# Sums of gated pairs on VectorE, an order laid out slot by slot, and four accumulators of the down product, in a hybrid decoder layer

## The chip, the core and the metric

The kernel runs on one core of one Trainium2 chip. The metric is the device time of one execution in microseconds. Three timed executions of the kernel before gave 2177.37, 2174.46 and 2172.34 us; the median is 2174.46 us.

The engines are named as in the profile: PE is TensorE (PEld its weight loads), DVE is VectorE, ACT is ScalarE, POOL is GpSimd, SP is the queue of SyncE that issues most loads. Each engine works through its own list of instructions in the order in which the program issued them; a wait on one instruction holds everything behind it on that engine.

## The reference, cut to what matters

One decoder layer on 512 positions of width 2048, in float32: an input projection, attention heads and state-space heads side by side, an output projection, and then the feed-forward part:

```python
x = x + jnp.concatenate([attn, ssm], axis=-1) @ w_out
h = rms_norm(x, norm2_w)
u = causal_dwconv(h @ w_up, ffn_conv_w, ffn_conv_b)      # w_up: 2048 x 11264
u_gate, u_val = jnp.split(u, 2, axis=-1)
return x + (jax.nn.silu(u_gate) * u_val) @ w_down        # w_down: 5632 x 2048
```

The change touches the last three lines alone: the up product with its convolution and gate, and the down product that is added to x.

## The kernel before, in words

Both products of the feed-forward part are done by a seven-product scheme for two-by-two blocks (Strassen's, in Winograd's form). A block of weights and a block of activations are cut in four, sums of the quarters are formed, and seven products P1 to P7 of the sums replace eight. Each factor is split in a high and a low part, and a product is made of three kinds of matmul: high by high (line 1265), high by low (1266) and low by high (1268).

**Groups, items, slots.** The up product has 44 groups (one of 128 gate columns with the 128 value columns that belong to them), the down product 24: three passes (over 8, 7 and 7 pairs of hidden blocks) of eight groups. A group has seven items, P1 to P7, and all items stand in one list, in which two groups are interleaved: P5 of group g, P3 of g-1, P1 of g, P4 of g-1, P6 of g, P2 of g, P7 of g. The place in that list is the slot. An item has 24 matmuls of 128x256 where the group works over 8 blocks (the up product and the first pass of the down product), and 21 where it works over 7.

**What a slot does.** The main loop issues an item's matmuls, then what reads its product out of PSUM (`up_after` or `down_after`), and then what the table `events` holds for that slot (`run`), the high part of the item three slots on (`split`, ScalarE, line 1038), the low part of the item two slots on (`split_lo`, VectorE, line 1047), and one step of the gate's work (`side`). So the order on each engine is set by the slot numbers given to `at`, and within a slot by the order of these calls.

**Sums of weights.** Per group the four quarters "11", "12", "21" and "22" of the weights are loaded (SP's queue, line 1007; quarter 22 a second time as "22b"), into two buffers `rawb` (for 21) and four buffers `rawa`. VectorE makes s1 = 21 + 22 (line 1021), s2 = s1 - 11 (1025) and s4 = 12 - s2 (1027) in the PSUM tile `s`; GpSimd makes s3 = 11 - 21 in place in `rawb` (line 1014). P5 is made from s1, P6 from s2, P3 from s4, P7 from s3; P1, P2 and P4 from 11, 12 and 22b. With p5 the slot of the group's P5, s1 is issued in slot p5-5, s3 in p5-2, s2 in p5 and s4 in p5+4.

**Gate's work.** Per up group VectorE scales the product rows (`ug`, `uv`, lines 1192 and 1193), runs the convolution (line 1174, with a first step on ScalarE, 1173) and multiplies gate and value into half of the tile `gt` (line 1185). After every second group, when `gt` holds a pair of hidden blocks, GpSimd makes the pair's four sums in three instructions (`sums`, lines 879 to 881) and stores the tile in `gd` in DRAM (line 1190).

**Down product.** Each pass first loads the pair sums back from `gd` (`b_load`, GpSimd's queue, line 1077, into the tiles `ld`; three buffers in the first pass, six later) and splits them in high and low parts `cmb` (`b_split`: ScalarE 1088, VectorE 1089), fourteen times per pass in the first sixteen slots counted from `base`, the P5 of the group ahead of the pass. `down_after` adds each product into the accumulator `acc_s` of the group (line 1144). The accumulator is loaded by GpSimd's queue (`down_acc`) from x (`x2d`, line 1206) or from what the pass before stored (`pd`, line 1208), one slot ahead of the group's P5, into one of two buffers, and stored (line 1053) one slot after the group's P4.

## Time and profile before

| | |
|---|---|
| median of the three times | 2174.46 us (2172.34 to 2177.37) |
| profiled execution, own time | 2176.35 us |
| its span, first to last instruction | 2174.7 us |
| PE, PEld busy | 2096.7 us (96%), 1966.4 us (90%) |
| DVE busy | 1645.8 us (76%) |
| ACT busy | 985.7 us (45%) |
| POOL busy | 363.0 us (17%) |
| mean granted TensorE clock | 0.989 of full speed |

The profiled execution is 1.65 us longer than its span, and 1.9 us above the median. The shares are averages over stages with different limits: the first 820 us are the mixer, the next 840 us the up product, the last 500 us the down product. Rows of a timeline give the start, the duration, the engine, line and operation, out<-in with the shape, and, in brackets, how long the engine had been idle before it and what released it. An instruction's recorded duration overlaps the next one's by some 0.08 us on VectorE; what it takes of the engine's time is read from start to start. Some matmul records are missing, so counts of them serve as shares, not as exact numbers.

### The profile page before, as it was taken

Reading aid. Unit: us, or ns where it says so; the run is one execution under the profiler, and the core shown is the slowest. Engines: PE = TensorE matmul, PEld = TensorE weight load, DVE = VectorE, ACT = ScalarE, POOL = GpSimd, SP = SyncE. Lnnn points to the kernel's source line nnn. Section 1 sums busy time; section 2 is a strip of 40 time slices with the busy share of each in tenths; the row PEclk is TensorE's granted clock in tenths of the full one; section 3 lists DMA queues with packets and bytes.
Section 4 is the critical chain, followed back from the end, with each engine's and each line's share of the span. In section 5 each row is a group of like instructions: output and inputs, shape, how many; then the busy total and the mean of one; then the engine's idle time right before and its main releaser. Section 6 shows DMA issues by size and latency. Waiting matters only on the chain.

```text
span 2174.7 us, 37764 instructions
## 1 busy us (share of the span) xinstructions
PE 2096.7 (96%) x15366; PEld 1966.4 (90%) x15366; DVE 1645.8 (76%) x2185; ACT 985.7 (45%) x1433; POOL 363.0 (17%) x293
## 2 busy tenths in 40 slices
PE   9999999999999989999999999999999899899798
PEld 7988888888888879999999999999999799899798
DVE  6545555345655559999999999999999867877776
ACT  5433445334444445544454554544455433434432
POOL 0010000000000011222212212222232322213111
PEclk9999999999999999999999999999999999999999
DMA  5232222232225444444444444444445556657553
GB/s 195 75 106 86 77 79 78 88 107 88 68 97 180 160 168 146 167 154 165 165 146 167 154 162 159 158 153 165 155 163 206 209 186 224 220 207 238 194 195 125
DMA packets 97406, 328.20 MB, mean 151 GB/s; under 512 B 10704, under 2 KB 15120, under 8 KB 94416
## 3 DMA queue, kind: packets, MB, share of 16 engines
q1 hardware_dynamic: 81424, 257.36, 34.9%
q0 software_dynamic: 15808, 68.43, 8.5%
q8 instruction: 121, 1.98, 0.4%
q14 instruction: 53, 0.43, 0.1%
HBM read 283.77 MB, written 41.98 MB: 150 GB/s over the span
## 4 chain that ended last, share of the span: by engine, by line
PE 72%; issue 12%; DVE 9%; DMA 3%; POOL 3%; ACT 1%; POOLq 0%; SPq 0%; DVEq 0%; ACTq 0%
PE acc L184 29%; PE x L1268 12%; PE x L1265 12%; PE x L1266 11%; PE sm L184 4%; DVE lo L1047 4%; POOL rawb L1014 1%; PE y L1266 1%; PE y L1265 1%; PE y L1268 1%; DVE s L1027 1%; DVE ug L1192 1%; DVE cmb L1089 1%; DMA acc_s<-pd 1%; DMA pd<-acc_s 1%
## 5 line engine op out<-in xcount | busy, mean ns | idle before, releaser
L1265 PE MATMUL x<-cmb,hi 128*128 128x256 f32 x3168 | 764.1, 281 | 26.0 <-DVE acc_s L1144 20.8
L1266 PE MATMUL x<-cmb,hi 128*128 128x256 f32 x3168 | 761.9, 281 | 8.7 <-DVE cmb L1089 8.3
L1265 PEld LDWEIGHTS x<-cmb,hi 128*128 128x128 f32 x3168 | 604.8, 191 | 29.2 <-issue 17.7
L1266 PEld LDWEIGHTS x<-cmb,hi 128*128 128x128 f32 x3168 | 605.4, 191 | 10.1 <-DVE cmb L1089 9.3
L1268 PE MATMUL x<-cmb,lo 128*128 128x256 f32 x3168 | 442.6, 282 | 30.6 <-DVE lo L1047 30.1
L1268 PEld LDWEIGHTS x<-cmb,lo 128*128 128x128 f32 x3168 | 401.9, 191 | 38.7 <-DVE lo L1047 38.5
L184 DVE TENSOR_TENSOR lo<-raw,hi 128x512 fp32r<-128x512 f32 (+1 forms) x240 | 164.4, 691 | 246.7 <-ACT hi L184 232.1
L184 PE MATMUL acc<-A,hi 128*128 128x512 f32 x704 | 281.1, 399 | 0.9 <-ACT hi L184 0.9
L1038 ACT ACTIVATE hi<-s 128x1024 fp32r<-128x1024 f32 (+1 forms) x201 | 200.8, 999 | 171.0 <-DVE s L1025 60.7
L184 PE MATMUL acc<-A,lo 128*128 128x512 f32 x704 | 277.7, 395 | 0.1
L1038 ACT ACTIVATE hi<-rawa 128x1024 fp32r<-128x1024 f32 (+1 forms) x204 | 210.5, 1032 | 146.6 <-PE x L1266 133.7
L184 PE MATMUL acc<-B,hi 128*128 128x512 f32 x704 | 276.9, 393 | 0.0
L184 ACT ACTIVATE hi<-raw 128x512 fp32r<-128x512 f32 (+1 forms) x240 | 150.3, 629 | 261.5 <-PE acc L184 228.5
L1047 DVE TENSOR_TENSOR lo<-rawa,hi 128x1024 fp32r<-128x1024 f32 (+1 forms) x204 | 251.1, 1231 | 0.0
L1014 POOL TENSOR_TENSOR rawb<-rawa,rawb 128x1024 f32<-128x1024 f32 (+1 forms) x68 | 160.9, 2367 | 465.8 <-DMA rawa<-wu 216.3
L1047 DVE TENSOR_TENSOR lo<-s,hi 128x1024 fp32r<-128x1024 f32 (+1 forms) x201 | 237.2, 1180 | 0.0
L1155 ACT ACTIVATE cP<-x 128x256 f32<-128x256 f32 x132 | 50.9, 385 | 318.4 <-PE x L1268 318.4
L184 PEld LDWEIGHTS acc<-A,lo 128*128 128x128 f32 x704 | 132.1, 188 | 32.4 <-DVE lo L184 1.5
L184 PEld LDWEIGHTS acc<-A,hi 128*128 128x128 f32 x704 | 132.7, 188 | 29.1 <-ACT hi L184 1.3
L184 PEld LDWEIGHTS acc<-B,hi 128*128 128x128 f32 x704 | 132.5, 188 | 28.7 <-DVE B L184 0.4
L1144 DVE TENSOR_TENSOR acc_s<-x,acc_s 128x256 f32<-128x256 f32 x144 | 60.8, 422 | 117.7 <-PE x L1268 56.1
L1047 DVE TENSOR_TENSOR lo<-rawb,hi 128x1024 fp32r<-128x1024 f32 (+1 forms) x68 | 137.3, 2019 | 0.0
(209 smaller groups left out, 3071.4 us busy)
## 6 DMA issues: line engine op xcount, KB each, us to landing
rawa<-wu SPq DMA_DIRECT2D x176, 512.0 KB, 4.1
raw<-wi SPq DMA_DIRECT2D x79, 512.0 KB, 3.5
rawa<-wdb SPq DMA_DIRECT2D x64, 448.0 KB, 4.2
rawb<-wu SPq DMA_DIRECT2D x44, 512.0 KB, 3.3
gd<-gt POOLq DMA_DIRECT2D x22, 1024.0 KB, 4.2
raw<-wo SPq DMA_DIRECT2D x32, 512.0 KB, 3.3
rawa<-wda SPq DMA_DIRECT2D x32, 512.0 KB, 4.2
ld<-gd POOLq DMA_DIRECT2D x26, 512.0 KB, 6.2
```

The costliest lines, as they stand in the source:

```text
L184: return fn(out, *args, **kw)
L1014: po.tensor_tensor(r, raw[gi, "11"][:, :n], r, op=OP.subtract)
L1027: ve.tensor_tensor(s_, raw[gi, "12"][:, :n], s_, op=OP.subtract)
L1038: se.activation(h[:, :n], src[:, :n], AF.Copy)
L1047: ve.tensor_tensor(l[:, :n], src[:, :n], h[:, :n].bitcast(F32), op=OP.subtract)
L1089: ve.tensor_tensor(lo, ld[:, :m, :], hi.bitcast(F32), op=OP.subtract)
L1144: ve.tensor_tensor(a[:, row, half], src, a[:, row, half], op=op)
L1155: se.activation(g[x], X[:, 256:] if x == "P5" else X[:, :256], AF.Copy)
L1192: yield lambda: ve.tensor_tensor(ug[:, 2:514], ug[:, 2:514], rbc, op=OP.mult)
L1265: pe.matmul(out, w, bk[:, 0, q, :], start=fresh and q == 0, stop=False, skip_group_check=True)
L1266: pe.matmul(out, w, bk[:, 1, q, :], start=False, stop=False, skip_group_check=True)
L1268: pe.matmul(out, l[:, q * 128:(q + 1) * 128], bk[:, 0, q, :], start=False, stop=q == n - 1, skip_group_check=True)
```

## The change

It moves the three instructions of the pair sums from GpSimd to VectorE, in two parts in different slots. Gate steps no longer come from a list of which one is taken per slot; each has a slot of its own. A second table `after` is run later in the slot: a slot now runs `events`, then the low part (`split_lo`), then `after` (s1, s3, `b_split`, the gate's steps, the pair sums), then the high part (`split`). s1 and s3 of a group stand together in slot p5-3, s4 in p5+5. In the down product all groups from the third on take their accumulator from four buffers `acc` in another pool, loaded in slot p5-6 (p5-2 for the third); the first and second keep `acc_s`, loaded in p5-2 and p5-5. The `ld` tiles of the second and third pass are five instead of six.

```diff
-    def sums(E, g):
-        E.tensor_tensor(g[:, 4:6, :], g[:, 1:4:2, :], g[:, 0:2, :], op=OP.subtract)
-        E.tensor_tensor(g[:, 6, :], g[:, 3, :], g[:, 4, :], op=OP.subtract)
-        E.tensor_tensor(g[:, 7, :], g[:, 2, :], g[:, 6, :], op=OP.subtract)
+    def sums(E, g, part=None):
+        if part != 1:
+            E.tensor_tensor(g[:, 4:6, :], g[:, 1:4:2, :], g[:, 0:2, :], op=OP.subtract)
+        if part != 0:
+            E.tensor_tensor(g[:, 6, :], g[:, 3, :], g[:, 4, :], op=OP.subtract)
+            E.tensor_tensor(g[:, 7, :], g[:, 2, :], g[:, 6, :], op=OP.subtract)
...
-        at(p5 - 5 if gi != 1 else 0, add, gi, "s1"), at(pos[gi, "P7"] - 8 if gi else -3, add, gi, "s3")
-        at(max(p5 - 1, p6 - 4), add, gi, "s2"), at(p6, add, gi, "s4")
+        if gi:
+            at(p5 - 3 if gi > 1 else 1, add, gi, "s1", where=after)
+            at(p5 - 3 if gi > 1 else 1, add, gi, "s3", where=after)
+        else:
+            at(-5, add, gi, "s1"), at(-3, add, gi, "s3")
+        at(max(p5 - 1, p6 - 4), add, gi, "s2"), at(pos[gi, "P3"] - 3, add, gi, "s4")
...
-        box["depth"] = 6
+        box["depth"] = 5
...
-        early = 5 if p == 0 else 6
+        early = 5
         for q in range(14):
-            at(base + slots[q], b_split, k0 + q)
+            at(base + slots[q], b_split, k0 + q, where=after)
         for q in range(14):
-            at(base - 6 + q // 2 if q < early else base + slots[q - early if p else q - 3] + 1, b_load, k0 + q)
+            at(base - 6 + q // 2 if q < early else base + slots[q - (5 if p else 3)] + 1, b_load, k0 + q)
         if p == 0:
-            at(base + 21, down_pool)
+            at(base + 19, down_pool)
...
-                sums(po, box["gt"])
+        def t_sums(n):
+            sums(ve, box["gt"], n)
+            if n:
...
                 po.dma_start(gd[p][:, pr - PASSES[p][0]], box["gt"])
...
+        t0 = pos[i, "P4"]
+        for d, fn in ((0, lambda: ve.tensor_tensor(ug[:, 2:514], ug[:, 2:514], rbc, op=OP.mult)),
+                      (1, lambda: ve.tensor_tensor(uv[:, 258:514], uv[:, 258:514], rbc[:, 256:], op=OP.mult)),
+                      (3, lambda: conv(ug, i, "tg", 0)), (4, lambda: conv(ug, i, "tg", 1)), (5, val0),
+                      (6, lambda: conv(uv, NF + i, "tv", 1)), (6, last)):
+            at(t0 + d, fn, where=after)
+        if i % 2:
+            at(t0 + 7, t_sums, 0, where=after), at(t0 + (10 if i < NF - 1 else 8), t_sums, 1, where=after)
...
-        a = g["acc"] = side_tile(lp, [2, S], "acc_s", 2)
+        if gi < NF + 2:
+            a = g["acc"] = side_tile(lp, [2, S], "acc_s", 2)
+        else:
+            a = g["acc"] = side_tile(box["pool"], [2, S], "acc", 4)
...
-            at(pos[gi, "P5"] - 1, down_acc, gi)
+            p5 = pos[gi, "P5"]
+            at(p5 - 2 if gi == NF else p5 - 5 if gi == NF + 1 else p5 - 2 if gi == NF + 2 else p5 - 6, down_acc, gi)
...
+    def step_slot(slot):
+        run(slot)
+        if slot > -3:
+            split_lo(slot + 2)
+        run(slot, after)
+        split(slot + 3)
```

The first place is VectorE's list in the up product, after a pair of groups is complete. Before, from the product that fills `gt` (the tiles `lo`, `hi`, `rawa`, `rawb` and `s` are those of the weights, `ug`, `uv`, `tg`, `tv` those of the gate, `x` and `y` the PSUM products):

```order
L1185 TENSOR_TENSOR gt<-tg,tv 128x512
L1163 TENSOR_TENSOR uv_7164<-x,rbc 128x256
L1047 TENSOR_TENSOR lo_11013<-rawa,hi_10980 128x1024
L1192 TENSOR_TENSOR ug_7162<-ug_7162,rbc 128x512
L1027 TENSOR_TENSOR s<-rawa,s 128x1024
L1047 TENSOR_TENSOR lo_11047<-rawb,hi_11011 128x1024
L1193 TENSOR_TENSOR uv_7164<-uv_7164,rbc 128x256
L1157 TENSOR_TENSOR ug_7158<-y,cP_10974 128x256
L1047 TENSOR_TENSOR lo_11081<-s,hi_11045 128x1024
```

And in the changed kernel, from the first of the pair's sums on (line 880; 882 and 883 are the other two, 1023 is s1, 1029 is s4, 1049 the low part):

```order
L880 TENSOR_TENSOR gt<-gt 128x512
L1201 TENSOR_TENSOR ug_7158<-ug_7158,rbc 128x512
L1049 TENSOR_TENSOR lo_11278<-rawb,hi_11248 128x1024
L1023 TENSOR_TENSOR s<-rawb,rawa 128x1024
L1202 TENSOR_TENSOR uv_7160<-uv_7160,rbc 128x256
L1163 TENSOR_TENSOR ug_7162<-y,cP_11209 128x256
L1029 TENSOR_TENSOR s<-rawa,s 128x1024
L1049 TENSOR_TENSOR lo_11315<-s,hi_11284 128x1024
L1165 TENSOR_TENSOR uv_7164<-x,cP_11144 128x256
L1049 TENSOR_TENSOR lo_11348<-s,hi_11317 128x1024
L882 TENSOR_TENSOR gt<-gt 128x256
L883 TENSOR_TENSOR gt<-gt 128x256
```

The sums are new in this list. s1 (1023) now stands right ahead of the short product of `uv` and of a run of instructions that read `y`, `x` or `s`, which are PSUM tiles; s3, which GpSimd can start once s1 has read `rawb`, falls beside that run.

The second place is VectorE's list where the up product ends and the first pass of the down product begins, in the slot of the first down group's P6. Before and, in the second fence, in the changed kernel (`cmb<-ld` is `b_split`, 1089 and now 1096; the accumulator's lines are 1144 and now 1150):

```order
L1144 TENSOR_TENSOR acc_s<-x,acc_s 128x256
L1027 TENSOR_TENSOR s<-rawa,s 128x1024
L1089 TENSOR_TENSOR cmb_17735<-ld,cmb_17735 128x1024 x2
L1047 TENSOR_TENSOR lo_17744<-rawb,hi_17702 128x1024
L1193 TENSOR_TENSOR uv_7164<-uv_7164,rbc 128x256
```

```order
L1150 TENSOR_TENSOR acc_s<-x,acc_s 128x256
L1049 TENSOR_TENSOR lo_17737<-rawb,hi_17706 128x1024
L1023 TENSOR_TENSOR s<-rawb,rawa 128x1024
L1096 TENSOR_TENSOR cmb_17742<-ld,cmb_17742 128x1024 x2
L1202 TENSOR_TENSOR uv_7164<-uv_7164,rbc 128x256
```

The low part of a later item now comes ahead of the two splits of loaded sums, not behind them, and s1 stands between.

The third place is GpSimd's list in the first pass of the down product (`x2d_148` and `x2d_149` are loaded into the accumulator of the fifth group; `pd_2` is the store of the third). Before:

```order
L1053 DMA pd_1_7059<-acc_s 128x1024
L1014 TENSOR_TENSOR rawb<-rawa,rawb 128x1024
L1206 DMA acc_s<-x2d_146 128x512
L1206 DMA acc_s<-x2d_147 128x512
L1053 DMA pd_2_7060<-acc_s 128x1024
L1014 TENSOR_TENSOR rawb<-rawa,rawb 128x1024
L1206 DMA acc_s<-x2d_148 128x512
L1206 DMA acc_s<-x2d_149 128x512
```

In the changed kernel:

```order
L1218 DMA acc<-x2d_146 128x512
L1218 DMA acc<-x2d_147 128x512
L1056 DMA pd_1_7059<-acc_s 128x1024
L1016 TENSOR_TENSOR rawb<-rawa,rawb 128x1024
L1218 DMA acc<-x2d_148 128x512
L1218 DMA acc<-x2d_149 128x512
L1056 DMA pd_2_7060<-acc 128x1024
L1016 TENSOR_TENSOR rawb<-rawa,rawb 128x1024
```

An accumulator's load now stands ahead of the store and of the sum that were issued before it, and goes into a buffer of its own rather than into the one that the store has just been issued from.

More of the change, by code (lines that the diff above doesn't have):

```diff
@@ L1048, in split_lo, with at @@
         parts[k] = (h, l)
-    events = {}
-    def at(slot, fn, *args):
-        events.setdefault(slot, []).append(lambda: fn(*args))
+    events, after = {}, {}
+    def at(slot, fn, *args, where=events):
+        where.setdefault(slot, []).append(lambda: fn(*args))
     for gi in range(len(groups)):
@@ L1128, in body @@
         at(slot, x_split, n)
-    side = []
     box = {}
@@ L1163, in up_after @@
             ve.tensor_tensor(uv[:, 2:258], X[:, :256], rbc[:, :256], op=OP.mult)
-            side.extend(up_side(i, ug, uv))
+            up_side(i, ug, uv)
     def up_side(i, ug, uv):
@@ L1230, in body, with run @@
     at(1, lambda: stat_bc(box["ps"].tile([128, 512], F32, name="y")))
-    def run(slot):
-        for fn in events.pop(slot, ()):
-            fn()
-    def before(lo, hi):
-        for slot in range(lo, hi):
-            run(slot)
-            split(slot + 3)
-            if slot > -3:
-                split_lo(slot + 2)
+    def run(slot, where=events):
+        for fn in where.pop(slot, ()):
+            fn()
+    def step_slot(slot):
[4 more added lines that the diff above has]
+        split(slot + 3)
     for slot in range(min(events), -3):
         run(slot)
-    before(-3, -2)
+    step_slot(-3)
     while gens:
@@ L1250, in body @@
                                                reuse_waits="tile"))
-    before(-2, 0)
+    step_slot(-2), step_slot(-1)
     for k, (gi, x) in enumerate(items):
@@ L1272, in body @@
         (up_after if g["ph"] == "up" else down_after)(g, x)
-        run(k)
-        split(k + 3)
-        split_lo(k + 2)
-        if side:
-            side.pop(0)()
+        step_slot(k)
     for slot in sorted(events):
```

8 lines of the change are left out of this document (removed).

## The prediction

> **What bounds the kernel now.** I first read the stages: the busy times of the engines in stretches of the span. The columns are PE, PEld, DVE, ACT and POOL busy time with their instructions, the granted TensorE clock, and DMA.
>
> ```profile
> core 0: us, PE busy (x) PEld busy (x) DVE busy (x) ACT busy (x) POOL busy (x), PEclk, DMA share, GB/s
> 905.00:1623.00 718.00, 701.66 (x6047) 698.12 (x6046) 702.67 (x757) 358.00 (x468) 168.39 (x108) 1.00 0.44 159
> 1660.00:1760.00 100.00, 81.47 (x605) 78.31 (x604) 80.34 (x89) 44.05 (x48) 31.23 (x31) 0.90 0.54 191
> 1760.00:1840.00 80.00, 80.00 (x697) 80.00 (x696) 59.10 (x70) 30.24 (x30) 21.16 (x22) 1.00 0.63 225
> 1840.00:1900.00 60.00, 52.98 (x421) 51.91 (x421) 50.03 (x60) 29.95 (x33) 14.67 (x16) 0.94 0.59 207
> 1960.00:2080.00 120.00, 107.06 (x874) 104.66 (x873) 92.41 (x113) 50.27 (x56) 30.42 (x32) 0.97 0.65 222
> ```
>
> The stretch 1760 to 1840, inside the first pass of the down product, is TensorE's own pace: never idle, full clock, 697 recorded matmuls in 80 us, 0.1148 us each. At that pace 1660 to 1760 would hold 871 matmuls and held 605, so 30.5 us are lost; 1840 to 1900 holds 421, worth 48.3 us, so 11.7 are lost; 1960 to 2080 holds 874, worth 100.3, so 19.7 are lost. These are the starts of the three passes. In the up product (first row) DVE is busier than PE: 702.67 of 718 us.
>
> The pace of a group is seen in the accumulator's additions, which follow the products. Each row stands for the same product one group later (first pair: groups over 8 blocks; second: over 7).
>
> ```profile
> 1763.36 0.42 DVE L1144 TENSOR_TENSOR acc_s<-x,acc_s 128x256 f32<-128x256 f32 x1 [1.16 <-PE x L1268]
> 1782.72 0.43 DVE L1144 TENSOR_TENSOR acc_s<-x,acc_s 128x256 f32<-128x256 f32 x1 [1.16 <-PE x L1268]
> ...
> 2135.85 0.42 DVE L1144 TENSOR_TENSOR acc_s<-x,acc_s 128x256 f32<-128x256 f32 x1 [0.42 <-PE x L1268]
> 2152.79 0.43 DVE L1144 TENSOR_TENSOR acc_s<-x,acc_s 128x256 f32<-128x256 f32 x1 [0.97 <-PE x L1268]
> ```
>
> So TensorE needs 19.36 us for a group over 8 blocks (2.77 per slot) and 16.94 over 7 (2.42 per slot). VectorE waits for PE here, so nothing else sets this pace. In the up product a pair of groups could take 38.72 us. GpSimd's timeline shows what it takes, and the operations that VectorE meets:
>
> ```profile
> 905.18 1.29 POOL L879 TENSOR_TENSOR gt<-gt 128x512 f32<-128x512 f32 x1 [17.48 <-DVE gt L1185]
> ...
> 1243.83 2.41 POOL L1014 TENSOR_TENSOR rawb<-rawa,rawb 128x1024 f32<-128x1024 f32 x1 [12.01 <-ACT hi L1038]
> 1268.72 0.57 POOL L1190 DMA_DIRECT2D gd<-gt  x1 [0.30 <-POOL gt L881]
> 1269.31 2.41 POOL L1014 TENSOR_TENSOR rawb<-rawa,rawb 128x1024 f32<-128x1024 f32 x1
> ...
> 1623.40 1.29 POOL L879 TENSOR_TENSOR gt<-gt 128x512 f32<-128x512 f32 x1 [18.06 <-DVE gt L1185]
> ```
>
> From 905.18 to 1623.40 lie 18 pairs: 39.90 us each, 1.18 over TensorE's pace. VectorE's timeline of one such pair says why:
>
> ```profile
> 1243.62 1.21 DVE L1047 TENSOR_TENSOR lo<-s,hi 128x1024 fp32r<-128x1024 f32 x1
> 1244.75 2.04 DVE L1185 TENSOR_TENSOR gt<-tg,tv 128x512 f32<-128x512 f32 x1
> ...
> 1263.54 0.69 DVE L1185 TENSOR_TENSOR gt<-tg,tv 128x512 f32<-128x512 f32 x1
> 1265.08 1.60 DVE L1047 TENSOR_TENSOR lo<-rawa,hi 128x1024 fp32r<-128x1024 f32 x1
> 1266.60 1.22 DVE L1192 TENSOR_TENSOR ug<-ug,rbc 128x512 f32<-128x512 f32 x1
> 1268.88 3.93 DVE L1047 TENSOR_TENSOR lo<-rawb,hi 128x1024 fp32r<-128x1024 f32 x1
> ```
>
> The same `gt` product takes 0.69 us alone and 2.04 where GpSimd's s3 (1243.83 to 1246.24) runs; the low part of `rawb` takes 3.93 us beside the s3 at 1269.31. But the low part at 1243.62, which reads the PSUM tile `s`, keeps its 1.21 under the same s3. So GpSimd's sums stop a VectorE instruction that reads two SBUF tiles, and not one that reads PSUM.
>
> In the down product the waits say what is late; the second and third entries are VectorE's:
>
> ```profile
> PE x L1265 <- DVE acc_s L1144: 20.8, 9, 5.0
> DVE acc_s L1144 <- DMA acc_s<-pd: 33.9, 12, 4.9
> DVE acc_s L1144 <- DMA acc_s<-x2d: 18.7, 4, 8.1
> ```
>
> **The change, part by part.** *Up product.* VectorE's 702.67 us are 39.04 per pair. GpSimd's stops in the pair above are 2.04-0.69, 1.60-1.21, 1.22-0.68 and 3.93-1.21, together 5.00 us (the 0.68 is the row at 1698.56 below). Without them VectorE has 34.04 us of work. The pair sums come onto it: one 128x512, two 128x256. The nearest rows are `gt` alone (0.69) and the accumulator's 0.42, so 1.53 us; the same sums of the mixer's `gx` tiles on VectorE bound it above:
>
> ```profile
> L184 DVE TENSOR_TENSOR gx<-gx 128x512 f32<-128x512 f32 x8 | 7.6, 950 | 1.8 <-ACT gx L184 1.8
> ```
>
> That is 0.95+0.84, 1.79 us; from start to start (0.08 less each) 1.3 is the lower end. I take 1.53, since 950 ns is a mean over a place where other work interferes: 35.6 us per pair against TensorE's 38.72. VectorE no longer bounds the pair, if s3 stops nothing. In the new order s3 can start only when s1 is done; what then stands on VectorE is one product of two SBUF tiles (`uv`, L1202), then s4, two low parts and two sums that all read PSUM: about 4 us, longer than s3's 2.41. Nothing of the five microseconds is left but the `uv` product's case. When both start together, VectorE has won:
>
> ```profile
> 1698.56 0.68 DVE L1192 TENSOR_TENSOR ug<-ug,rbc 128x512 f32<-128x512 f32 x1
> 1698.57 2.92 POOL L1014 TENSOR_TENSOR rawb<-rawa,rawb 128x1024 f32<-128x1024 f32 x1
> ```
>
> It is VectorE that keeps its 0.68 and GpSimd that takes 0.5 longer. The `uv` product starts right behind s1, and GpSimd's s3 needs the message that s1 is done, so I take no stop; the ends are 0 and 2.72 us per group. Within a slot the most VectorE work is s2, a low part and a convolution step, 1.13+1.13+0.66 from start to start, 2.9 us beside a slot of 2.77, and the next slots are shorter; TensorE reads a low part only two slots on. s1 itself, two slots later than before, is ready 2.3 us after the end of P6 on TensorE, its high part 1.05 later, and TensorE wants it after two more items, 5.5 us: 2.1 us are left. So the up product should run at TensorE's pace: 18 x 1.18 = 21.2 us gained. The pair before 905 and the transition are not in this.
>
> The Trainium skill, SBUF — State Buffer, "Who interferes with whom", says that VectorE and GpSimd share a port pair by an exclusive lock and that whoever issues first has it for the whole instruction. The row at 1698.57 agrees, the row at 1268.88 does not: that low part started 0.43 us ahead of the s3 at 1269.31 and still ended after it (it had started behind the descriptor work of 1268.72, which by the page should not hold it). By the rule the `uv` product wins and the sum is as above; by that row it loses 2.72 us in every group, which is the second rival below.
>
> *Down product, accumulators.* Before, an accumulator's load waits on GpSimd's queue until the store from the same buffer has landed. In the first transition:
>
> ```profile
> 1707.67 1.09 POOL L1206 DMA_DIRECT2D acc_s<-x2d  x2
> 1716.73 0.42 DVE L1144 TENSOR_TENSOR acc_s<-x,acc_s 128x256 f32<-128x256 f32 x1 [5.04 <-DMA acc_s<-x2d]
> 1739.79 0.58 POOL L1206 DMA_DIRECT2D acc_s<-x2d  x1 [4.42 <-DMA pd<-acc_s]
> 1743.77 0.42 DVE L1144 TENSOR_TENSOR acc_s<-x,acc_s 128x256 f32<-128x256 f32 x1 [8.07 <-DMA acc_s<-x2d]
> acc_s<-x2d POOLq DMA_DIRECT2D x16, 256.0 KB, 4.2
> ```
>
> Four buffers and six slots of lead (16.6 us, or 14.5 over 7 blocks) cover even the 9.1 us from 1707.67 to 1716.73. The third group has two slots and its own item, 8.3 us, against a landing of 4.2: covered, if GpSimd comes to it in time. What queues behind the early load on GpSimd, a store and s3, does not wait longer, since the buffer is free four groups ahead. So I drop these waits. What is left of each transition is VectorE's work, which the early load doesn't touch.
>
> *First transition.* In the 17 slots from the first `b_split` to the last pair sum, the new order gives VectorE 38 instructions of 128x1024 (1.13 us from start to start), 21 of 128x256 (0.34), 9 convolution steps (0.66) and 7 others of 128x512 (0.60): 60.1 us. TensorE needs 17 x 2.77 = 47.0. VectorE falls 13.1 us behind; it may lag 2.4 (one slot less an addition) before TensorE waits; and s3 may fall between two `b_split` in a row, which read two SBUF tiles, 2.4 more. So 13.1 of the 30.5 us stay and 17.4 are gained.
>
> *The other two.* Over 7 blocks the rows are
>
> ```profile
> L1047 DVE TENSOR_TENSOR lo<-rawa,hi 128x896 fp32r<-128x896 f32 x48 | 51.9, 1082 | 0.0
> L1089 DVE TENSOR_TENSOR cmb<-ld,cmb 128x768 fp32r<-128x768 f32 x14 | 13.9, 994 | 0.0
> ```
>
> A group has ten of the first size (1.00 from start to start) and seven additions: 12.4 us. The fourteen `b_split` are 7 x 1.13 + 7 x 0.87 = 14.0, spread over two groups: 38.8 us beside TensorE's 33.9, so 4.9 behind, less 2.4 of lag, plus 2.4 for the same s3: 4.9. At the start of the second pass one of the groups still has TensorE's longer items, which I put at 1.4 us more cover: 3.5. Gained: 11.7-3.5 and 19.7-4.9, together 23.0.
>
> Everything else (five `ld` tiles for six, steps of ScalarE placed ahead of the high part, s4 a slot later) I cost at nothing: ScalarE is busy 358 of 718 us in the up product, and s4's low part is still read two slots after it. Without that cover each would be a share of an item per group, as in the last rival.
>
> The sum: 21.2+17.4+23.0 = 61.6 us off. The profiled span becomes 2113.1, its execution 2114.8; against the median of 2174.46 it is 2112.9. I say 2112.
>
> **The rivals.** *The transitions keep more* (0.15). The waits show 20.8 us of TensorE directly behind the late accumulators; the rest of the 61.9 us lost (30.5+11.7+19.7) may come from the chain of `b_load`, where a buffer freed by VectorE is loaded one or two slots ahead of use:
>
> ```profile
> POOL ld L1077 <- DVE cmb L1089: 83.1, 25, 11.5
> ```
>
> The change leaves that chain as it is in the first pass and with a buffer less in the others. Then 21.2+20.8 = 42.0 are gained: 2132. Against it, VectorE, not a load, was at work in 80.34 of the 100 us.
>
> *s3 stops the `uv` product* (0.10). With 2.72 us per group VectorE has 35.6+5.4 = 41.0 per pair, 1.1 more than today: the up product loses 20 instead of gaining 21, and the down product still gains 40.4: 2154. It decides once the stop passes 1.6 us.
>
> *The loads are early in the order and not in time* (0.05). GpSimd takes its queue in order and stands behind `b_load`s in the first transition; then 5.04 and 8.07 stay: 2125.
>
> *Slower* (0.04). s1 now stands 2.1 us ahead of need with ScalarE's high part behind it, in order. If it were late by more in each group, through its two loads or through VectorE's lag, each microsecond beyond would cost TensorE one in each of the 43 up groups that have this slot; from 3.6 us late on (1.5 x 43 = 64.5) the gain is gone: 2177. Against it, the two loads are asked for six slots ahead.
>
> **How the numbers follow.** The forecast has 0.66; its own range is 2099 (the transitions lose half of what I count) to 2124. With the first and third rival 2098 to 2142 holds a little over eight in ten; 2154 and the slower case are left out. A difference of 0.2%, 4.3 us, is about what a measurement of this kernel can tell from none. Only the last rival is slower: faster 0.94, within 0.2% 0.02, slower 0.04.
>
> **What would show it.** The stops are gone: the `gt`, `ug` and `rawb` rows at 0.69, 0.68 and 1.21, pairs 38.7 us apart, s3 about 2.6 us long and the `uv` product 0.41. A `uv` product near 3 us, or pairs at 39.9 or more, would be the second rival. In the down product the accumulator's waits for DMA vanish; the starts of the passes lose about 13, 4 and 5 us, with VectorE busy in them; ScalarE or VectorE waiting for `ld` there would be the first rival. An idle TensorE behind the high part of P5 in every up group would make the prediction wrong altogether.

## The result and the profile after

The changed kernel takes 2127.01 us (median; 2125.47 to 2128.22), the kernel before 2174.34 (2171.68 to 2177.37) beside it. The ratio is 0.9783, with a 95% interval of 0.9770 to 0.9795. The direction and the range hold, but 47 us are gained where 62 were counted.

The page of the changed kernel gives its span and busy times:

```profile
span 2125.4 us, 37670 instructions
PE 2081.9 (98%) x15366; PEld 1958.4 (92%) x15366; DVE 1584.6 (75%) x2251; ACT 987.9 (46%) x1433; POOL 283.4 (13%) x227
```

The stages of the changed kernel, with the columns of the prediction's first fence (us of the span; PE, PEld, DVE, ACT and POOL busy with instructions; granted clock; DMA share; GB/s): the up product, then the starts of the three passes.

```profile
908.00:1605.00 697.00, 697.00 (x6051) 697.00 (x6050) 650.55 (x811) 362.54 (x469) 98.40 (x54) 1.00 0.46 164
1640.00:1740.00 100.00, 86.12 (x684) 83.48 (x684) 86.52 (x104) 47.01 (x51) 27.46 (x27) 0.95 0.61 211
1820.00:1880.00 60.00, 57.07 (x485) 56.08 (x484) 53.20 (x67) 31.15 (x35) 19.37 (x19) 1.00 0.70 240
1960.00:2060.00 100.00, 95.86 (x799) 94.80 (x798) 84.43 (x106) 44.10 (x50) 25.55 (x25) 0.97 0.65 219
```

In the up product TensorE is never idle now, and VectorE is busy 650.55 of 697 us where it had been busy 702.67 of 718. The starts of the passes are still thin: at 0.1148 us a matmul the 684, 485 and 799 leave 21.5, 4.3 and 8.3 us lost.

To see where each microsecond went, I compare the start of the same VectorE instruction in two traces: the `gt` product of the second and of the twentieth pair, and the addition of P1 in the 3rd, 14th and 21st down group. VectorE's timeline of the kernel before, and then of the changed kernel:

```profile
904.43 0.67 DVE L1185 TENSOR_TENSOR gt<-tg,tv 128x512 f32<-128x512 f32 x1
1622.64 0.68 DVE L1185 TENSOR_TENSOR gt<-tg,tv 128x512 f32<-128x512 f32 x1
1749.61 0.42 DVE L1144 TENSOR_TENSOR acc_s<-x,acc_s 128x256 f32<-128x256 f32 x1 [1.68 <-PE x L1268]
1962.46 0.43 DVE L1144 TENSOR_TENSOR acc_s<-x,acc_s 128x256 f32<-128x256 f32 x1 [0.97 <-PE x L1268]
2102.05 0.42 DVE L1144 TENSOR_TENSOR acc_s<-x,acc_s 128x256 f32<-128x256 f32 x1
```

```profile
907.78 0.69 DVE L1191 TENSOR_TENSOR gt<-tg,tv 128x512 f32<-128x512 f32 x1
1604.74 0.69 DVE L1191 TENSOR_TENSOR gt<-tg,tv 128x512 f32<-128x512 f32 x1
1721.14 0.42 DVE L1150 TENSOR_TENSOR acc<-x,acc 128x256 f32<-128x256 f32 x1
1925.98 0.42 DVE L1150 TENSOR_TENSOR acc<-x,acc 128x256 f32<-128x256 f32 x1 [0.98 <-PE x L1281]
2052.76 0.42 DVE L1150 TENSOR_TENSOR acc<-x,acc 128x256 f32<-128x256 f32 x1 [0.98 <-PE x L1281]
```

Row by row the changed kernel is 3.4 us later, then 17.9, 28.5, 36.5 and 49.3 earlier. The differences of these numbers are the gains of the stages. The table has them for every kernel of this document, against the same trace of before. (Each comes from one profiled execution. At the start, traces whose order is the same there differ by up to 1.8 us, so a microsecond in that column means little; in the up product they agree within 0.1, in the first transition within 0.7. The medians were taken in five batches, with the kernel before at 2173.8 to 2176.9 us; between batches they compare to within some 3 us.)

| Gain in us | start, to 2nd pair | up, 18 pairs | first transition | second | third | median us |
|---|---|---|---|---|---|---|
| forecast | 0 | 21.2 | 17.4 | 8.2 | 14.8 | 2112 |
| the changed kernel | -3.4 | 21.3 | 10.6 | 8.0 | 12.8 | 2127.0 |
| without s3 | 0.5 | 21.3 | 13.2 | 7.9 | 15.5 | 2119.1 |
| sums on GpSimd | -2.9 | 21.3 | 5.5 | 7.9 | 13.8 | 2130.7 |
| s1, s3, s4 in old slots | -2.5 | 20.8 | 13.5 | 3.1 | 12.2 | 2130.6 |
| s1, s3 ahead of the low part | -5.2 | 0.0 | 5.9 | 4.9 | 12.6 | 2158.7 |
| second group's s1, s3 at old place | -1.1 | 21.3 | 9.9 | 6.1 | 15.7 | 2124.1 |
| three s3 behind the loads | -2.5 | 21.3 | 12.1 | 7.9 | 15.7 | 2122.7 |
| third accumulator a slot earlier | -2.3 | 21.3 | 14.4 | 4.7 | 15.7 | 2123.3 |
| these last three together | -2.0 | 21.3 | 17.6 | 7.9 | 15.7 | 2115.4 |
| sums and s1, s3, s4 as before | -2.7 | -0.8 | 8.7 | 2.8 | 12.3 | 2157.3 |
| accumulators as before | -4.0 | 21.3 | 5.2 | -19.7 | -7.7 | 2185.3 |
| only the accumulators changed | -1.8 | 0.1 | 8.0 | 7.2 | 14.7 | 2148.7 |
| three together, 4 splits doubled | -1.9 | 21.3 | 11.5 | 7.9 | 15.5 | 2121.4 |

The second line against the first: the up product and the second transition are as forecast; the first transition lacks 6.8 us, the third 2.0, and the start loses 3.4 that were not in the sum.

**The up product.** The two `gt` products of the changed kernel above, at 907.78 and 1604.74, stand 18 pairs apart: 38.72 us each. VectorE's groups by line (busy us, mean ns of one) show that the `gt` product and the `uv` product are not stopped, on the mean of all 44; one pair's timeline shows the place of s3.

```profile
L1191 DVE TENSOR_TENSOR gt<-tg,tv 128x512 f32<-128x512 f32 x44 | 30.4, 692 | 1.5
L1202 DVE TENSOR_TENSOR uv<-uv,rbc 128x256 f32<-128x256 f32 x44 | 18.4, 418 | 0.0
```

```profile
1242.88 0.42 DVE L1202 TENSOR_TENSOR uv<-uv,rbc 128x256 f32<-128x256 f32 x1
1243.12 2.45 POOL L1016 TENSOR_TENSOR rawb<-rawa,rawb 128x1024 f32<-128x1024 f32 x1 [13.29 <-DVE s L1023]
1243.59 1.22 DVE L1029 TENSOR_TENSOR s<-rawa,s 128x1024 f32<-128x1024 f32 x1
```

s3 comes 0.24 us behind the `uv` product, which keeps its 0.42; what follows on VectorE reads PSUM and keeps its 1.22.

**The start.** Here s1 and s3 of the second group stand in slot 1, and there VectorE's next but one instruction reads two SBUF tiles (timelines of VectorE and GpSimd in the changed kernel):

```profile
813.31 3.33 POOL L1016 TENSOR_TENSOR rawb<-rawa,rawb 128x1024 f32<-128x1024 f32 x1 [7.88 <-DVE s L1023]
814.30 3.42 DVE L1049 TENSOR_TENSOR lo<-rawb,hi 128x1024 fp32r<-128x1024 f32 x1
```

A low part that takes 1.22 alone takes 3.42.

**The first transition.** From the timelines of VectorE, GpSimd, ScalarE and TensorE in the changed kernel:

```profile
1677.74 2.35 DVE L1096 TENSOR_TENSOR cmb<-ld,cmb 128x1024 fp32r<-128x1024 f32 x2
1677.97 4.73 POOL L1016 TENSOR_TENSOR rawb<-rawa,rawb 128x1024 f32<-128x1024 f32 x1 [2.31 <-DVE s L1023]
1682.64 1.52 POOL L1084 DMA_DIRECT2D ld<-gd  x2
1687.80 1.06 ACT L1095 ACTIVATE cmb<-ld 128x1024 fp32r<-128x1024 f32 x1 [4.76 <-DMA ld<-gd]
1688.91 0.58 PE L1278 MATMUL x<-cmb,hi 128*128 128x256 f32 x1 [3.08 <-ACT cmb L1095]
...
1706.10 2.44 POOL L1016 TENSOR_TENSOR rawb<-rawa,rawb 128x1024 f32<-128x1024 f32 x1 [3.63 <-DVE s L1023]
1706.32 2.50 DVE L883 TENSOR_TENSOR gt<-gt 128x256 f32<-128x256 f32 x1
1709.12 0.58 POOL L1198 DMA_DIRECT2D gd<-gt  x1 [0.58 <-DVE gt L883]
1709.70 2.14 POOL L1218 DMA_DIRECT2D acc<-x2d  x4
1717.07 0.42 DVE L1150 TENSOR_TENSOR acc<-x,acc 128x256 f32<-128x256 f32 x1 [4.19 <-DMA acc<-x2d]
```

Two things are late. First, two `b_split` in a row hold s3 off: it ends at 1682.70 instead of about 1680.4, and only then come the two loads queued behind it; ScalarE waits 4.76 us for the data and TensorE 3.08 for ScalarE. Second, GpSimd comes to the third group's accumulator at 1709.70, and VectorE waits 4.19 for it. Ahead of that load stands the last store of the pair sums, and it was held up by an s3 as well: the s3 at 1706.10 stops the last pair sum, which takes 2.50 us instead of 0.42. The loads issued there then land 5.5 to 7.0 us after their issue (the view of tile `acc`, 1695 to 1730 us).

### The profile page after: what moved, and what is told of

The parts are those of the page before. It is cut to its first block, busy times and chain, and to the rows that moved or that the text cites. A ratio compares the mean times of both kernels' runs of the same rounds, so it can differ in the third digit from the quotient of the medians.

```text
span 2125.4 us, 37670 instructions
## 1 busy us (share of the span) xinstructions
PE 2081.9 (98%) x15366; PEld 1958.4 (92%) x15366; DVE 1584.6 (75%) x2251; ACT 987.9 (46%) x1433; POOL 283.4 (13%) x227
## 4 chain that ended last, share of the span: by engine, by line
PE 88%; DVE 5%; issue 3%; DMA 2%; ACT 1%; POOL 1%; POOLq 0%; SPq 0%; DVEq 0%; ACTq 0%
PE acc L184 30%; PE x L1281 16%; PE x L1279 15%; PE x L1278 15%; PE sm L184 4%; PE y L1281 2%; PE y L1278 2%; PE y L1279 2%; DVE lo L1049 1%; DMA ld<-gd 1%; DVE cmb L1096 1%; POOL rawb L1016 0%; DVE lo L184 0%; DVE s L1023 0%; DMA acc<-x2d 0%
## 5 line engine op out<-in xcount | busy, mean ns | idle before, releaser
L1281 PE MATMUL x<-cmb,lo 128*128 128x256 f32 x3168 | 436.2, 280 | 6.3 <-DVE lo L1049 6.3
L1016 POOL TENSOR_TENSOR rawb<-rawa,rawb 128x1024 f32<-128x1024 f32 (+1 forms) x68 | 169.3, 2490 | 927.1 <-DVE s L1023 723.8
L1049 DVE TENSOR_TENSOR lo<-rawa,hi 128x1024 fp32r<-128x1024 f32 (+1 forms) x204 | 241.3, 1183 | 0.0
L1040 ACT ACTIVATE hi<-rawa 128x1024 fp32r<-128x1024 f32 (+1 forms) x204 | 209.5, 1027 | 39.1 <-PE x L1279 38.9
L184 PE MATMUL acc<-hi,A 128*128 128x256 f32 (+2 forms) x448 | 135.4, 302 | 0.7 <-DVE u L184 0.7
L184 PE MATMUL acc<-lo,A 128*128 128x256 f32 (+2 forms) x448 | 133.5, 298 | 0.0
```

The source lines that it names most:

```text
L184: return fn(out, *args, **kw)
L1016: po.tensor_tensor(r, raw[gi, "11"][:, :n], r, op=OP.subtract)
L1040: se.activation(h[:, :n], src[:, :n], AF.Copy)
L1049: ve.tensor_tensor(l[:, :n], src[:, :n], h[:, :n].bitcast(F32), op=OP.subtract)
L1281: pe.matmul(out, l[:, q * 128:(q + 1) * 128], bk[:, 0, q, :], start=False, stop=q == n - 1, skip_group_check=True)
```

## The experiments

My theory of what is missing (14 us by the medians, 12 in the table): it is three collisions of the new order (s3 at the start, s3 with the loads behind it in the transitions, the third accumulator), not the terms of the sum. The rival: VectorE's own work in the transitions is more than I counted. A first group of runs takes the up product's two edits apart, a second the three collisions, a third the accumulators.

**Without s3.** It leaves out the sum s3 for all groups (P7 then multiplies another operand), so part of the computation is missing.

```diff
-            po.tensor_tensor(r, raw[gi, "11"][:, :n], r, op=OP.subtract)
```

> The changed kernel without GpSimd's s3 at all (P7 multiplies quarter 21 itself, so the output is not the reference's). Theory: in the up product's steady pairs s3 is hidden already, so pairs stay at 38.72 us; what the prediction missed (3.4 us at the start of the up product, about 6.8 us in the first transition, 2.1 in the third) is s3 meeting VectorE instructions with two SBUF inputs there, and delaying the loads queued behind it. Without s3 that comes back: 2113 to 2120 us. Rival: the transitions are longer because VectorE's own work there was counted too low; then only the directly blocked instructions come back (2.2 + 2.1 + 1.9 us) and the time is 2121 to 2125.

2119.06 us (ratio 0.9745, 0.9730 to 0.9760). The up product gains nothing by it: s3 is hidden there. The start gets 3.9 us back, the first transition 2.6 and the third 2.7, together 9.2 of the 12.2 us missing in the table. The first transition still lacks 4.2; VectorE waits 6.18 us there for the third group's accumulator.

**Sums back on GpSimd, the new order kept.**

```diff
-            sums(ve, box["gt"], n)
+            sums(po, box["gt"], n)
```

> The changed kernel with the pair sums back on GpSimd, in their new slots. Theory A (the order round s3 is what frees the pair; VectorE has 3 us to spare): the sums stop VectorE by 2.5 to 3.5 us per pair instead of costing it 1.5, 36.5 to 37.5 us of 38.72, pairs stay at 38.7 to 38.8 and the time at 2125 to 2131. Theory B (the move of the sums is what pays): pairs go back to 39.3 or more, 2138 to 2150.

2130.68 us (0.9798, 0.9784 to 0.9813). The pairs stay at 38.72, and the up product keeps its 21.3 us; the time that is lost against the changed kernel is lost in the first transition (5.5 instead of 10.6).

**The sums on VectorE, s1, s3 and s4 in their old slots.**

```diff
-            at(p5 - 3 if gi > 1 else 1, add, gi, "s1", where=after)
-            at(p5 - 3 if gi > 1 else 1, add, gi, "s3", where=after)
...
-        at(max(p5 - 1, p6 - 4), add, gi, "s2"), at(pos[gi, "P3"] - 3, add, gi, "s4")
+        at(p5 - 5 if gi != 1 else 0, add, gi, "s1"), at(pos[gi, "P7"] - 8 if gi else -3, add, gi, "s3")
+        at(max(p5 - 1, p6 - 4), add, gi, "s2"), at(p6, add, gi, "s4")
```

> The changed kernel with s1, s3 and s4 in the slots and at the place within the slot that they had before; the sums stay on VectorE. Theory A: s3 falls beside a convolution step and the gate's product again and stops VectorE 1.3 to 2.7 us per group; at 1.3 the pair needs 38.2 us of VectorE (time 2122 to 2131, since the collision at the start of the up product also goes), at 2.7 it needs 41.0 (2165). Theory B (moving the sums alone pays): 2122 to 2128, pairs at 38.72.

2130.56 us (0.9801, 0.9785 to 0.9818). Again the pairs stay at 38.7. The stage 1000 to 1600 us, first of the kernel with the sums on GpSimd, then of this one:

```profile
1000.00:1600.00 600.00, 600.00 (x5209) 600.00 (x5208) 549.99 (x652) 311.95 (x404) 125.53 (x91) 1.00 0.46 163
```

```profile
1000.00:1600.00 600.00, 600.00 (x5205) 599.88 (x5204) 590.58 (x697) 311.90 (x403) 83.39 (x46) 1.00 0.47 163
```

600 us are 15.5 pairs: VectorE needs 35.5 us per pair in the one, less than the 36.5 to 37.5 that I had expected, and 38.1 in the other. Both are under TensorE's 38.72, so both give the whole 21 us. Either edit is enough in the up product; with the new order kept, the sums on VectorE even cost it a little (36.1 in the changed kernel).

**Both undone.** The last two edits at once.

> The changed kernel with the pair sums on GpSimd and s1, s3 and s4 in their earlier slots, both undone at once; the gate's fixed slots, the low part ahead of the gate's steps and the early accumulators stay. Theory: the pair has a threshold, VectorE's need with its stops against TensorE's 38.72 us; either edit alone brings it under (the two runs with one undone have pairs of 38.7), neither leaves it above: pairs at 39.5 to 40 us again, 14 to 23 us lost against the changed kernel, 2143 to 2151. Rival: the gate's fixed slots alone are enough: pairs at 38.7, 2130 to 2134.

2157.29 us (0.9920, 0.9905 to 0.9935), the pairs at 39.94: neither edit, no gain. So the pair has a threshold, and the effects of the two edits don't add. (VectorE is busy 584.37 of the 600 us from 1000 to 1600, 38.9 us per pair, which is only 0.2 over 38.72; it also waits for TensorE's products, 12.1 us in that stretch or 0.8 per pair, and together they come near the 39.94.) I expected at most 2151; the other 6 us are lost in the transitions, 1.9 in the first and 5.2 in the second, as with s1 and s3 in their old slots alone (4.9 in the second).

**s1 and s3 one step earlier within their slot**, ahead of the low part:

```diff
-            at(p5 - 3 if gi > 1 else 1, add, gi, "s1", where=after)
-            at(p5 - 3 if gi > 1 else 1, add, gi, "s3", where=after)
+            at(p5 - 3 if gi > 1 else 1, add, gi, "s1", where=events)
+            at(p5 - 3 if gi > 1 else 1, add, gi, "s3", where=events)
```

> The changed kernel with s1 and s3 one step earlier within the same slot, ahead of the low part of rawb, so that two instructions with two SBUF inputs (the low part, 1.13 us, and the uv product, 0.34) stand behind s1 instead of one. Theory A (whoever waits gets the pair when the first instruction ends): s3 starts after the low part and the uv product is stopped for about 2.4 us per group: VectorE 40.4 us per pair, 2155 to 2170. Theory B (VectorE keeps the pair through back-to-back instructions, as it did with two splits in a row in two of three transitions): s3 takes 3.8 us instead of 2.4, nothing stops, pairs at 38.72, 2123 to 2131.

2158.71 us (0.9926, 0.9911 to 0.9941). The timelines of VectorE and GpSimd in one of its groups:

```profile
1233.40 1.22 DVE L1049 TENSOR_TENSOR lo<-rawb,hi 128x1024 fp32r<-128x1024 f32 x1
1233.63 3.25 POOL L1016 TENSOR_TENSOR rawb<-rawa,rawb 128x1024 f32<-128x1024 f32 x1 [16.67 <-DVE s L1023]
1234.54 2.62 DVE L1202 TENSOR_TENSOR uv<-uv,rbc 128x256 f32<-128x256 f32 x1
```

Now s3 meets the low part, gets its turn when that ends, and the `uv` product takes 2.62 us. (41 of the 44 take 2.62 or 2.63.) This is what the prediction's second rival describes: pairs at 39.9, the up gain gone, even with the sums on VectorE. One place within a slot is worth 21 us.

**The start.** s1 and s3 of the second group back in their earlier slots:

```diff
-            at(p5 - 3 if gi > 1 else 1, add, gi, "s1", where=after)
-            at(p5 - 3 if gi > 1 else 1, add, gi, "s3", where=after)
+            if gi > 1:
+                at(p5 - 3, add, gi, "s1", where=after)
+                at(p5 - 3, add, gi, "s3", where=after)
+            else:
+                at(0, add, gi, "s1"), at(pos[gi, "P7"] - 8, add, gi, "s3")
```

> The changed kernel with s1 and s3 of the second group back in their earlier slots (0 and eight slots ahead of P7); nothing else is changed. Theory: the 3.4 us that the changed kernel loses ahead of the first pair come from this one s3, now beside a low part of two SBUF tiles: the first pair's gt product comes about 3.4 us earlier than in the changed kernel, and the whole is about 3.4 us shorter, 2123.6. Rival: the start is lost to the order of the gate's steps there, which this edit leaves as it is: 2127, the first pair unchanged.

2124.09 us (0.9768, 0.9754 to 0.9783). The stretches 800 to 840 us of the kernel before, of the changed kernel and of this one:

```profile
800.00:820.00 20.00, 19.96 (x146) 19.72 (x146) 15.06 (x20) 11.51 (x16) 4.34 (x2) 0.82 0.68 236
820.00:840.00 20.00, 20.00 (x175) 20.00 (x175) 17.21 (x21) 9.49 (x12) 2.41 (x1) 1.00 0.38 132
```

```profile
800.00:820.00 20.00, 18.48 (x127) 18.04 (x127) 13.62 (x16) 9.05 (x12) 5.28 (x2) 0.80 0.61 201
820.00:840.00 20.00, 19.27 (x166) 19.07 (x166) 17.11 (x21) 10.07 (x14) 2.47 (x1) 1.00 0.38 129
```

```profile
800.00:820.00 20.00, 19.66 (x138) 19.22 (x138) 13.69 (x19) 11.16 (x14) 4.33 (x2) 0.81 0.69 229
820.00:840.00 20.00, 20.00 (x176) 20.00 (x175) 17.14 (x20) 9.01 (x13) 2.47 (x1) 1.00 0.40 138
```

Of 28 matmuls missing (321 before, 293 after, 3.2 us) 21 are back, 2.4 us; the `gt` product of the second pair is 2.3 us earlier, where 3.4 were expected. But this is one trace against one. The same stretch holds 304 in the two later kernels with this edit (three together, splits doubled), and 288 to 299 in the four with the changed start. By the table's first column the edit is worth 1.3 us on the mean (1.7 late against 3.0). So the theory holds for a part, and the rest of the loss stays open: the kernel with only the accumulators changed, whose order at the start is that of before, is 1.8 late as well.

**s3 behind the loads.** In the second, tenth and eighteenth down group s3 stands one slot later:

```diff
-            at(p5 - 3 if gi > 1 else 1, add, gi, "s3", where=after)
+            at(p5 - 2 if gi in (NF + 1, NF + 9, NF + 17) else p5 - 3 if gi > 1 else 1, add, gi, "s3", where=after)
```

> s3 of the second, tenth and eighteenth group of the down product one slot later, behind the loads that stood behind it on GpSimd and out of the slot with two b_split in a row; nothing else is changed. Theory: what the transitions keep beyond VectorE's work is s3 held up by the splits (4.73 us in the first) and the loads of the next sums that queue behind it; TensorE's stretch from 1680 to 1700 us of the first transition fills, 4 to 6 us in all are gained, 2121 to 2123. Rival 1: VectorE's own work sets the transition, and s3's place changes only which of its instructions is stopped: 2126 to 2128. Rival 2: s3 one slot later makes P7's operand late, each time by about the 2.4 us of the sum: 2129 or more.

2122.67 us (0.9761, 0.9745 to 0.9778): within the theory's bounds. 1.5 us come from the first transition and 2.9 from the third (which other runs gained without this edit, as the next one shows). In the first, the last `gt` product is 2.8 us earlier, and half of that is lost again at the third accumulator, which is as late as it was (VectorE waits 4.29 us for it).

**The third accumulator a slot earlier**, with the pool's opening and the last pair's second sums ahead of it:

```diff
-            at(base + 19, down_pool)
+            at(base + 18, down_pool)
...
-            at(t0 + 7, t_sums, 0, where=after), at(t0 + (10 if i < NF - 1 else 8), t_sums, 1, where=after)
+            at(t0 + 7, t_sums, 0, where=after), at(t0 + (10 if i < NF - 1 else 7), t_sums, 1, where=after)
...
-            at(p5 - 2 if gi == NF else p5 - 5 if gi == NF + 1 else p5 - 2 if gi == NF + 2 else p5 - 6, down_acc, gi)
+            at(p5 - 2 if gi == NF else p5 - 5 if gi == NF + 1 else p5 - 3 if gi == NF + 2 else p5 - 6, down_acc, gi)
```

> The last pair's second part of the sums one slot earlier, the pool of the four accumulators opened one slot earlier, and the third down group's accumulator loaded one slot earlier; nothing else is changed. Theory: the 4.19 us that VectorE waits for that load, and the 2.13 us that TensorE then waits, vanish: 2 to 4 us are gained, 2123 to 2125. Rival: the next late thing (the sums that b_load brings) takes the place of this wait: 2126 to 2128.

2123.26 us (0.9760, 0.9744 to 0.9776; single runs from 2117.97 to 2126.18). In its VectorE timeline the wait, now at 1711.87, is 1.34 us instead of 4.19, and the last pair sum, a slot away from s3, takes 0.43.

The first transition gains 3.8 us. The second loses 3.3 and the third wins 2.9 against the changed kernel, though no edit touches them. ScalarE, VectorE and GpSimd in the third transition show why, first in the changed kernel, then in the one with the start mended, whose code there is the same:

```profile
1986.30 3.99 DVE L1096 TENSOR_TENSOR cmb<-ld,cmb 128x1024 fp32r<-128x1024 f32 x2
1986.53 2.95 POOL L1016 TENSOR_TENSOR rawb<-rawa,rawb 128x896 f32<-128x896 f32 x1 [0.87 <-issue]
...
1986.53 0.84 ACT L1095 ACTIVATE cmb<-ld 128x768 fp32r<-128x768 f32 x1 [1.49 <-DMA ld<-gd]
```

```profile
1986.69 2.09 DVE L1099 TENSOR_TENSOR cmb<-ld,cmb 128x1024 fp32r<-128x1024 f32 x2
1986.92 3.85 POOL L1016 TENSOR_TENSOR rawb<-rawa,rawb 128x896 f32<-128x896 f32 x1 [0.87 <-issue]
...
1986.76 0.84 ACT L1098 ACTIVATE cmb<-ld 128x768 fp32r<-128x768 f32 x1 [1.53 <-DMA ld<-gd]
```

The two splits take 2.09 us, or 3.99 if s3 gets between them, and by this one pair of traces that moves the transition by 2.9 us. In these two it goes with how early the second split is ready. The first ends about 1.14 us after its start; ScalarE's high part for the second is done at 1987.37 in the first trace, 0.07 ahead of that moment, and at 1987.60 in the second, 0.23 ahead. That isn't the whole rule, as the last section shows. (In the second transition of the run above, the second split waited for its load, and s3 ran meanwhile.)

**The three together.** The last three edits at once.

> The three edits together: s1 and s3 of the second group at their earlier slots, s3 of three down groups behind the loads, the third down group's accumulator a slot earlier. Theory: the three causes lie in different places and add up, 3.4 at the start and 6 to 10 in the transitions: 2114 to 2118. Rival: the transitions are bound by VectorE's work, and only the start is gained: 2123 to 2124.

2115.39 us (0.9727, 0.9713 to 0.9742; runs from 2114.01 to 2117.19): the fastest kernel of this study, 12 us under the changed one. The transitions give 17.6, 7.9 and 15.7 us against the forecast's 17.4, 8.2 and 14.8. In the first the parts more than add up (1.5 + 3.8 = 5.3 singly, 7.0 together), as each alone ran into the other.

**The accumulators as before, the rest changed.**

```diff
-        if gi < NF + 2:
-            a = g["acc"] = side_tile(lp, [2, S], "acc_s", 2)
-        else:
-            a = g["acc"] = side_tile(box["pool"], [2, S], "acc", 4)
+        a = g["acc"] = side_tile(lp, [2, S], "acc_s", 2)
...
-            at(p5 - 2 if gi == NF else p5 - 5 if gi == NF + 1 else p5 - 2 if gi == NF + 2 else p5 - 6, down_acc, gi)
+            at(p5 - 1, down_acc, gi)
```

(`down_pool` is back at base + 21 as well.)

> The changed kernel with the accumulators as before: two buffers for all groups, loaded one slot ahead, the pool opened two slots later; five ld tiles stay. Theory: the waits of VectorE for the accumulators' loads return in all three transitions, with TensorE behind them (20.8 us before): 10 to 20 us lost, 2137 to 2147, the up product as in the changed kernel. Rival: VectorE's work in the new order sets the transitions, and the loads are hidden behind it: 2127 to 2132.

2185.25 us (1.0046, 1.0031 to 1.0061): 58 us lost, far outside both expectations, and slower than the kernel before. Not only the transitions lose but each group. GpSimd's and VectorE's timelines in the third pass:

```profile
2049.61 0.73 POOL L1056 DMA_DIRECT2D outT<-acc_s  x1 [13.98 <-DVE acc_s L1150]
2053.87 2.12 POOL L1016 TENSOR_TENSOR rawb<-rawa,rawb 128x896 f32<-128x896 f32 x1 [3.52 <-DVE s L1023]
2055.95 0.56 POOL L1217 DMA_DIRECT2D acc_s<-pd  x1
2062.73 0.42 DVE L1150 TENSOR_TENSOR acc_s<-x,acc_s 128x256 f32<-128x256 f32 x1 [5.26 <-DMA acc_s<-pd]
```

In the new order s3 waits for s1, and the load stands behind s3 on GpSimd's queue: it goes out 6.3 us after the store, and VectorE waits 5.26 for it. In the kernel before, s3 stood right behind the store and needed no wait, and the load waited only for the store to land, 4.2 us behind it (GpSimd's timeline, third pass):

```profile
2105.20 0.72 POOL L1053 DMA_DIRECT2D outT<-acc_s  x1 [11.21 <-DVE acc_s L1144]
...
2109.37 0.55 POOL L1208 DMA_DIRECT2D acc_s<-pd  x1 [1.29 <-DMA outT<-acc_s]
```

So the two parts of the change hang together: the new place of s1 and s3 needs the loads ahead of it.

**Only the accumulators changed**, in the order of before:

```diff
-        a = g["acc"] = side_tile(lp, [2, S], "acc_s", 2)
+        if gi < NF + 2:
+            a = g["acc"] = side_tile(lp, [2, S], "acc_s", 2)
+        else:
+            a = g["acc"] = side_tile(box["pool"], [2, S], "acc", 4)
...
-            at(pos[gi, "P5"] - 1, down_acc, gi)
+            p5 = pos[gi, "P5"]
+            at(p5 - 2 if gi == NF else p5 - 5 if gi == NF + 1 else p5 - 2 if gi == NF + 2 else p5 - 6, down_acc, gi)
```

(with five `ld` tiles and the pool's opening at base + 19.)

> The kernel before with the early accumulators alone: four buffers, six slots of lead, five ld tiles; order, sums and gate as before. Theory: pairs stay at 39.9, and the gain is what TensorE waited behind the late accumulators, at most 20.8 us: 2154 to 2166. Rival: the early loads alone bring nothing, since VectorE's work with its stops sets the transitions of the old order: 2170 to 2175.

2148.70 us (0.9874, 0.9858 to 0.9891). The pairs stay at 39.9, the three transitions give 29.9 us, nearly the 31.4 of the changed kernel. The total is 5 us under the expected range, and the 29.9 are 9 more than the 20.8 that I took for the most: TensorE's waits directly behind the accumulator's addition are not all that a late addition costs. (What stands behind it on VectorE comes late too; that share was not measured by itself.)

**Four splits doubled**, on the kernel with the three edits. The same low part is written twice, for the last four `b_split` of the first pass:

```diff
-        ve.tensor_tensor(lo, ld[:, :m, :], hi.bitcast(F32), op=OP.subtract)
+        for _ in range(2 if p == 0 and k - [x[0] for x in b_list].index(0) >= 10 else 1):
+            ve.tensor_tensor(lo, ld[:, :m, :], hi.bitcast(F32), op=OP.subtract)
```

> The kernel with the three edits together, and the low part of the last four b_split of the first pass computed twice (the same result written again): four more VectorE instructions of 128x1024 in the first transition, 1.13 us each from start to start. Theory: what the first transition still loses there is VectorE's own work, which TensorE follows at once: the whole 4.5 us are lost, 2119.5 to 2120.5, all of it between the last gt product and the third down group. Rival: loads or ScalarE set what is left, and the added work lies beside them: 0 to 1 us lost, 2115 to 2116.5.

2121.44 us (0.9745, 0.9728 to 0.9763), 6.0 us more. The stretch 1680 to 1700 us of the kernel with the three edits, and of this one:

```profile
1680.00:1700.00 20.00, 18.44 (x146) 17.99 (x146) 19.88 (x25) 10.96 (x12) 3.13 (x2) 0.94 0.49 173
```

```profile
1680.00:1700.00 20.00, 15.31 (x100) 14.60 (x99) 19.86 (x22) 9.94 (x11) 3.00 (x2) 0.84 0.50 171
```

All of it falls in the first transition (17.6 to 11.5): TensorE follows VectorE's work there, as the prediction had it. The other two transitions were not tested so. The size was 4.5 and is 6.1 by the traces (by the ratios, each against the kernel before in its own batch, 3.9): the last `gt` product is 4.8 us later, and the rest comes with a granted clock of 0.84 instead of 0.94.

## Why the prediction was right and where it was wrong

**The up product was right, in its mechanism and its size.** The sum had 21.2, the trace 21.3; VectorE's need was put at 35.6 us per pair and is 36.1 (650.55 of 697 us, 18 pairs of 38.72, in the changed kernel). The choice of no stop for the `uv` product holds: the 44 take 0.42 on the mean. What the prediction doesn't say, and the runs show, is that the 5.0 us of stops were far more than the 1.18 us to be gained, so either edit alone would do.

**"Everything else ... I cost at nothing" was wrong.** The sum began with the second pair, and "the pair before 905" was left out with no price. There s1 and s3 of the second group were moved as well, next to a low part of two SBUF tiles: the same collision that I had priced at 2.72 in a rival for the other groups. The low part is 2.2 us longer (3.42 against 1.22). What that costs is known roughly: kernels with this start are 2.3 to 4.0 us late there, those with the start mended 1.1 to 2.0. The five `ld` tiles, in the same sentence, were not tested alone.

**"Covered, if GpSimd comes to it in time" was wrong for the third group.** I had worked out the lead (8.3 us against a landing of 4.2) in slots. In the trace the lead is 3.2 us, from the issue at 1709.70 to 1712.88, when VectorE begins to wait, and the loads land after 5.5 to 7.0 us. I had not looked at what stands ahead of the load on GpSimd in that transition: the last store of the pair sums, which follows VectorE's lag and a pair sum that s3 had stopped for 2.1 us. This is the third rival, at one group instead of several; to load a slot sooner, with the pair's last sums moved as well, is worth 3.8 us.

**The s3 in the transitions was mis-sized.** I charged 2.4 us to VectorE for an s3 between two splits, once per transition. In the first transition the splits won and s3 was late instead, with two loads behind it: the chain of `b_load` of the first rival, set off by a sum. In the third it cost 2.9 or nothing, from trace to trace. What I set against the first rival, that VectorE was at work in 80.34 of 100 us, was too coarse: a busy engine does not say that nothing else is late in the other 20.

**The rest of the transitions came out right in sum, in part by luck.** With the three edits the transitions give 41.2 us where 40.4 were counted, and the doubled splits show that TensorE follows VectorE in the first of them. But the sum had charged 2.4 us for an s3 in each transition, 7.2 in all, and in that kernel s3 stops one VectorE instruction there, a split at 1681.76 that takes 1.69 us instead of 1.22. So some 6 us of the other terms (VectorE's work, the lag, what was put at nothing) were counted too low, much as the rival of the experiments had it; no run takes them apart. The sum of 61.6 is near what the change gives without its collisions, since the kernel with the three edits takes 2115.4 with 2.0 us still lost at the start, but it got there by two errors that cancel. The second rival and the slower one did not come, but the first of these is one place within a slot away.

## What to carry to other kernels

When work is moved in an order written by hand, price the moved instruction at every place where it lands, the first and last turns of the loop too, and go down the queue behind it: a sum that waits holds up the loads that follow it. A stop only counts as far as it lifts an engine over the one that sets the pace, so two cures for the same stop don't add. Move loads ahead of a waiting instruction first; here that, with five `ld` tiles for six, gave 26 us, and the new order without it lost 58 against the order with it.

## What was not expected of the hardware

When a GpSimd sum waits for VectorE, it isn't settled whether it gets in after VectorE's running instruction or only after the next one. In the third transition s3 took 2.95 us in one trace and 3.85 in the other, and there the second split's readiness went with it (0.07 us ahead, 0.23 ahead). But in the kernel with the accumulators as before s3 got in although both splits had been ready for long (ScalarE and VectorE in the second transition):

```profile
1861.70 1.93 ACT L1095 ACTIVATE cmb<-ld 128x1024 fp32r<-128x1024 f32 x2 [0.40 <-DMA ld<-gd]
1866.01 3.99 DVE L1096 TENSOR_TENSOR cmb<-ld,cmb 128x1024 fp32r<-128x1024 f32 x2
```

The second high part is done at 1863.63, some 3.5 us before the first split ends, and the two splits still take 3.99 us; its third transition shows the same. So readiness alone doesn't decide, and what does is open, for the `uv` product at 1234.54 too. The Trainium skill, SBUF — State Buffer, "Who interferes with whom", says that issue order decides who blocks, and that the pair of ports that the two engines share is held for the whole instruction. The trace agrees for the low part at 1233.40, which keeps its 1.22 us while s3 waits, and for the `uv` product behind it. It does not agree where the second of two splits, issued after s3, kept its time: at 1677.74 the two take 2.35 us and s3 takes 4.73.

A stall of TensorE can cost more than its length. With four splits doubled, the granted clock from 1680 to 1700 us was 0.84 instead of 0.94, and from 1700 to 1720, where TensorE was never idle, 0.94 instead of 1.00: 167 recorded matmuls against 174, 0.8 us. Of the 6.1 us lost about 1.3 are beyond VectorE's delay of 4.8.
